# Plain fp32 for the small products of a hybrid block (scores, values, gates), a mask added in PSUM, and other banks and steps for statistics

## The chip, the cores and the metric

The kernel runs on one core of a Trainium2 chip. The metric is the time of one execution on the device, in microseconds. Engines: TensorE (PE, matrix products; "PEld" are its weight loads), VectorE (DVE), ScalarE (ACT), GpSimd (POOL) and SyncE (SP, which issues the transfers). Each engine executes its own instructions in order; semaphores order the engines among each other.

## The reference

One layer of a hybrid block over 512 tokens (S) of width 2048 (D), in fp32. Its core, cut:

```python
mod = c_act @ w_ada + b_ada                       # six vectors: shift, scale, gate, twice
h = rms_norm(x, g_mix) * (1 + sc1) + sh1
xr, yr, q, k, v, f_logit = split(h @ w_in)        # 1024, 1024, 1024, 1024, 1024, 8
# recurrent group: 8 blocks of 128 channels
u = causal_depthwise_conv(xr)                     # 4 taps
r, i = sigmoid(block_diag(u, w_a) + b_a), sigmoid(block_diag(u, w_x) + b_x)
a = exp(-8 * r * softplus(-lam)); y_rec = scan(a, sqrt(1 - a * a) * (i * u)) * gelu(yr)
# attention group: 8 heads of 128, query blocks of 128
s = rms_norm(q) @ rms_norm(k).T / sqrt(128) + cum_q - cum_k     # cum: cumulative log of the forget gate
p = softmax(where(causal, s, -inf)); y_att = p @ v
x = x + gt1 * (concat(rms_norm(y_rec), rms_norm(y_att)) @ w_out)
h2 = rms_norm(x, g_ffn) * (1 + sc2) + sh2
gate, up = split(h2 @ w_up); x = x + gt2 * ((silu(gate) * up) @ w_down)
```

## The kernel before

**Split products.** Nearly every product is made from fp32 values that are split in two: a high part, which ACT copies in the rounded type fp32r (`R(...)` reinterprets an access as fp32r), and a low part, which DVE or POOL makes by subtraction. `mm` (L187) issues one fp32r product; a full product is three of them: high by high, high by low, low by high. Weights stream in through `raw` (two buffers), and are split into `whi`/`wlo` (three buffers each) on ACT (L182) and DVE (L183). A few small products are plain fp32: the sums and spreads of the statistics (L247, L256), the transposes (L470, L508), the bias sums.

**Stages.** In order: `w1` (the projection to `xr`, with the product for the modulation vectors `ada`/`adf` as long DVE steps L134/L144 beside it); the statistics of x (`rstd_x`: sums by products with ones, four columns copied, a power on POOL, a spread by products with the identity); `yr0` (a feature-major group, four PSUM banks); heads `h0` to `h7` (`tm_group`: 16 k-tiles x four token tiles x three products into 384 columns, 392 for head 0); `yr1`; `wo0` to `wo3` (output projection); `up0`, `up1` (two standard groups of the up projection) and then the rest of it in "fast chunks" `uf4` to `uf43`, whose weights and moving operands are sums of pieces made on DVE; `dn` (down projection).

**Attention inside projections.** Attention of head h runs beside the projection of head h+1 (of head 7 beside `yr1`): its steps are hooked after given k-tiles by `ATT_STEPS` (statistics of q and k, transposes of q and k, the four score blocks two by two, the transposes of the probabilities, the value products). A score block b is the product of 128 queries with (b+1) x 128 keys. Its bias is made ahead on ACT from the cumulative forget logits (L484), POOL adds the causal mask `dmask` to the last 128 columns (L485), and DVE's L498 adds the score from PSUM and takes the row's maximum (`nm`). The recurrent group works in pairs of blocks (`rec_pair`) hooked the same way in the stages of heads 3 to 6: `conv` loads a block of `xr` back, scales and filters it to `u`, splits u, loads the gates' weights `gw` and splits them to `gpg`; the gates and what follows (`carry`) run in the next head's stage.

**PSUM.** Eight banks of 128 x 512: four `acc` (projections), three `misc` and one `rg`. yr0 takes the four acc banks, as head 0 after it. Before a bank is taken again, its contents must have been copied out (L382 for yr0, L445 to L449 for a head, L498 for scores).

**Order.** A scheduler in the build orders each engine's instructions from priorities, from the program's order and from its own estimate of when operands are there; on the chip an engine then runs its list in order. `ahead` raises the priority of weight loads and splits, `EVAC` that of the copies out of a head's banks. In wo0, the statistics of the attention output are summed and spread at step 2, those of the recurrent output at step 5 (`MIXREC`), and `mix_rec` then scales the recurrent blocks. At the end of each standard up group `up_fin` takes the bias's sums and writes the activations (`up_out`).

## Time and profile before

| | us |
|---|---|
| Median of three runs | 2206.79 (2200.26 to 2207.86) |
| Profiled execution | 2206.86 |
| Its span | 2205.1 |
| TensorE busy | 2108.9 (96%) |
| VectorE busy | 1590.6 (72%) |
| ScalarE busy | 879.4 (40%) |
| GpSimd busy | 222.6 (10%) |

The profile is one execution recorded by the hardware. Its page lists busy time by engine, the span in 40 slices, the chain of work that ended last, and groups of instructions; the trace behind it answers for single stretches: windows (busy time of each engine in a stretch), waits (what an engine stood still for, by the event that ended the wait), lines (groups of equal instructions) and a timeline. [...] Ends of pipelined products are modelled, so the price of a product is read from start to start. A plain fp32 product leaves two records in the trace for one instruction.

### The profile page before, as it was taken

Reading aid. Unit: us, or ns where it says so; the run is one execution under the profiler, and the core shown is the slowest. Engines: PE = TensorE matmul, PEld = TensorE weight load, DVE = VectorE, ACT = ScalarE, POOL = GpSimd, SP = SyncE. Lnnn points to the kernel's source line nnn. Section 1 sums busy time; section 2 is a strip of 40 time slices with the busy share of each in tenths; the row PEclk is TensorE's granted clock in tenths of the full one; section 3 lists DMA queues with packets and bytes.
Section 4 is the critical chain, followed back from the end, with each engine's and each line's share of the span. In section 5 each row is a group of like instructions: output and inputs, shape, how many; then the busy total and the mean of one; then the engine's idle time right before and its main releaser. Section 6 shows DMA issues by size and latency. Waiting matters only on the chain.

```text
span 2205.1 us, 32703 instructions
## 1 busy us (share of the span) xinstructions
PE 2108.9 (96%) x12785; PEld 1915.9 (87%) x12785; DVE 1590.6 (72%) x2407; ACT 879.4 (40%) x1238; POOL 222.6 (10%) x169
## 2 busy tenths in 40 slices
PE   8987988888989999899999999999999999999999
PEld 6767887887878888799999999999999888888887
DVE  8997679887877779988888888888888443322332
ACT  5522336656543335544444444444444222221111
POOL 2260113333212310000000000000000000000000
PEclk9998999999999999999999999999999999999999
DMA  9968666665667862343444344443434985554443
GB/s 322 319 209 286 198 225 202 197 218 172 224 211 253 278 218 103 112 144 117 134 134 135 124 129 139 131 128 125 144 126 136 335 310 195 177 198 138 154 158 109
DMA packets 133021, 406.05 MB, mean 184 GB/s; under 512 B 14561, under 2 KB 19841, under 8 KB 123138
## 3 DMA queue, kind: packets, MB, share of 16 engines
q1 hardware_dynamic: 132866, 403.96, 54.6%
q8 instruction: 100, 1.64, 0.3%
q14 instruction: 55, 0.45, 0.1%
HBM read 361.15 MB, written 42.75 MB: 183 GB/s over the span
## 4 chain that ended last, share of the span: by engine, by line
PE 73%; DVE 12%; DMA 8%; ACT 3%; issue 2%; POOL 1%; SPq 0%; DVEq 0%; POOLq 0%; ACTq 0%
PE dn_0p L187 5%; PE dn_3p L187 5%; PE dn_2p L187 5%; PE dn_1p L187 5%; DMA ada<-in_adaT 2%; PE up0p L187 2%; PE wo2p L187 2%; PE wo3p L187 2%; PE wo1p L187 2%; DMA bw<-in_w 2%; DVE adf L144 2%; DVE ada L144 1%; PE uf5p L962 1%; PE uf42p L962 1%; PE uf35p L962 1%
## 5 line engine op out<-in xcount | busy, mean ns | idle before, releaser
L134 DVE SCALAR_TENSOR_TENSOR ada<-ada,c_b 128x1024 f32<-128x1024 f32 x128 | 165.9, 1307 | 46.3 <-DMA ada<-in_adaT 45.9
L183 DVE TENSOR_TENSOR uq_0tl<-uq_0r,uq_0th 128x1024 fp32r<-128x1024 f32 x40 | 49.0, 1225 | 63.9 <-ACT uq_0th L182 63.9
L182 ACT ACTIVATE uq_0sh<-uq_0r 128x1024 fp32r<-128x1024 f32 x40 | 42.5, 1061 | 89.5 <-PE uf23p L962 2.3
L183 DVE TENSOR_TENSOR uq_0al<-uq_0r,uq_0ah 128x1024 fp32r<-128x1024 f32 x40 | 49.0, 1225 | 40.1 <-ACT uq_0ah L182 40.1
L182 ACT ACTIVATE uq_1th<-uq_1ra 128x1024 fp32r<-128x1024 f32 x40 | 42.5, 1061 | 72.7 <-DVE uq_1ra L942 2.7
L182 ACT ACTIVATE uq_0th<-uq_0r 128x1024 fp32r<-128x1024 f32 x40 | 42.4, 1061 | 72.4 <-DVE uq_0r L942 1.9
L182 ACT ACTIVATE uq_1sh<-uq_1rb 128x1024 fp32r<-128x1024 f32 x40 | 42.5, 1062 | 70.5 <-PE uf43p L962 2.4
L182 ACT ACTIVATE uq_1ah<-uq_1ra 128x1024 fp32r<-128x1024 f32 x40 | 42.5, 1061 | 60.7 <-issue 59.2
L182 ACT ACTIVATE uq_0ah<-uq_0r 128x1024 fp32r<-128x1024 f32 x40 | 42.4, 1060 | 50.4 <-issue 46.8
L144 DVE SCALAR_TENSOR_TENSOR adf<-adf,c_b 128x1024 f32<-128x1024 f32 x32 | 56.4, 1763 | 2.3 <-DMA adf<-in_adaT 2.3
L183 DVE TENSOR_TENSOR uq_1tl<-uq_1ra,uq_1th 128x1024 fp32r<-128x1024 f32 x40 | 49.0, 1225 | 10.4 <-ACT uq_1th L182 10.4
L187 PE MATMUL w1p<-hph,w1h 128*128 128x512 f32 x128 | 48.7, 408 | 6.2 <-ACT hph L327 6.1
L187 PE MATMUL w1p<-hpl,w1h 128*128 128x512 f32 x128 | 52.1, 407 | 1.9 <-DVE hpl L328 1.6
L183 DVE TENSOR_TENSOR uq_0sl<-uq_0r,uq_0sh 128x1024 fp32r<-128x1024 f32 x40 | 49.0, 1226 | 4.0 <-ACT uq_0sh L182 0.4
L183 DVE TENSOR_TENSOR uq_1sl<-uq_1rb,uq_1sh 128x1024 fp32r<-128x1024 f32 x40 | 49.0, 1225 | 2.8 <-ACT uq_1sh L182 0.6
L187 PE MATMUL w1p<-hph,w1l 128*128 128x512 f32 x128 | 50.9, 398 | 0.0
L183 DVE TENSOR_TENSOR uq_1al<-uq_1ra,uq_1ah 128x1024 fp32r<-128x1024 f32 x40 | 48.6, 1216 | 0.1
L574 DVE SCALAR_TENSOR_TENSOR ba<-bw,sh,ba 128x512 f32<-128x512 f32 x45 | 33.2, 751 | 20.4 <-DMA bw<-in_w 17.0
L144 DVE SCALAR_TENSOR_TENSOR ada<-ada,c_b 128x1024 f32<-128x1024 f32 x32 | 41.2, 1287 | 3.7 <-DMA ada<-in_adaT 3.7
L183 DVE TENSOR_TENSOR dn_1l<-dn_2r,dn_1h 128x1024 fp32r<-128x1024 f32 x11 | 13.5, 1226 | 38.0 <-ACT dn_1h L182 38.0
L183 DVE TENSOR_TENSOR dn_1l<-dn_0r,dn_1h 128x1024 fp32r<-128x1024 f32 x11 | 13.5, 1226 | 37.6 <-ACT dn_1h L182 37.6
L183 DVE TENSOR_TENSOR dn_0l<-dn_2r,dn_0h 128x1024 fp32r<-128x1024 f32 x11 | 13.5, 1225 | 37.6 <-ACT dn_0h L182 37.6
(13854 smaller groups left out, 8430.9 us busy)
## 6 DMA issues: line engine op xcount, KB each, us to landing
ada<-in_adaT SPq DMA_DIRECT2D x160, 512.0 KB, 5.2
uq_0r<-in_wups SPq DMA_DIRECT2D x80, 512.0 KB, 4.1
uq_1ra<-in_wups SPq DMA_DIRECT2D x40, 512.0 KB, 4.0
uq_1rb<-in_wups SPq DMA_DIRECT2D x40, 512.0 KB, 3.2
adf<-in_adaT SPq DMA_DIRECT2D x32, 512.0 KB, 5.6
actd<-ach SPq DMA_DIRECT2D x44, 256.0 KB, 2.0
actd<-acl SPq DMA_DIRECT2D x44, 256.0 KB, 4.0
dn_0r<-in_wdown SPq DMA_DIRECT2D x11, 1024.0 KB, 4.9
```

The source lines that it names most:

```text
L134: nc.vector.scalar_tensor_tensor(out=t, in0=t, scalar=1.0, in1=cs, op0=ALU.mult, op1=ALU.mult, accum_out=ac)
L144: nc.vector.scalar_tensor_tensor(out=t, in0=t, scalar=1.0, in1=c_b[:, cs], op0=ALU.mult, op1=ALU.mult, accum_out=ada_acc[j][:, hf, i:i + 1])
L182: nc.scalar.activation(R(hi[:, :n]), raw_ap, AF.Copy)
L183: tail_lo.append(nc.vector.tensor_sub(R(lo[:, :n]), raw_ap, hi[:, :n]).ins)
L187: nc.tensor.matmul(ps, lhsT=R(l), rhs=R(r), start=start, stop=stop)
L574: nc.vector.scalar_tensor_tensor(out=ba[j], in0=src, scalar=s1, in1=ba[j], op0=ALU.mult, op1=ALU.add)
L962: nc.tensor.matmul(m[p], lhsT=R(w[:, ks]), rhs=R(x), start=first and p in opens, stop=last, skip_group_check=True)
```

## The change

- Scores: the transposed q and k are copied once, by ACT, and each score block is one plain fp32 product; the causal mask is added in PSUM by a second product, identity by mask, both rounded to fp32r once at the kernel's start. The DVE subtraction (L473) and the POOL mask addition (L485) go.
- Value products: v and the transposed probabilities are copied once and multiplied as plain fp32; the DVE subtractions L449 and L512 go.
- Gates: plain fp32 products of the loaded weights and u; the splits of both go.
- Steps: attention's steps come one to two k-tiles later (`ATT_STEPS`), with the score blocks in two pairs at steps 8 and 9; the forget logits' sums of head 0 at step 4, not 2.
- Banks: the w1 banks are copied out in another order, the statistics of x use acc banks, and yr0 uses the three misc banks and the rg bank.
- wo0: both sums at step 1, both spreads at step 4.
- The epilogue of the second standard up group (`up_out`) is issued after the first fast chunk's first half.

```diff
 YR0_AHEAD = 80
-MIXREC = 5
+FORGET_STEP = 4
+MIXREC_STEPS = (1, 4)
...
+    nc.scalar.activation(R(ident_r), ident, AF.Copy)
+    nc.scalar.activation(R(dmask_r), dmask, AF.Copy)
...
-    for f in range(8):
+    for f in (4, 5, 6, 7, 0, 1, 2, 3):
...
-    rstd_x = rstd_bcast(ssq_x, D, "rstd_x")
+    rstd_x = rstd_bcast(ssq_x, D, "rstd_x", bank=acc)
...
-    yr0 = fm_group(wyr[0], list(range(KT)), hp, "yr0", hooks=hk0, ahead=YR0_AHEAD)
+    yr0 = fm_group(wyr[0], list(range(KT)), hp, "yr0", hooks=hk0, ahead=YR0_AHEAD,
+                   ps=[misc(f"yr0p{f}") for f in range(3)] + [rgp("yr0p3")])
...
-            nc.scalar.activation(R(vh[:, t, :]), ps[t][:, 256:384], AF.Copy)
-            nc.vector.tensor_sub(R(vl[:, t, :]), ps[t][:, 256:384], vh[:, t, :])
+            nc.scalar.activation(v[:, t, :], ps[t][:, 256:384], AF.Copy)
...
-                nc.scalar.activation(R(hi), pt, AF.Copy, scale=g)
-                nc.vector.scalar_tensor_tensor(out=R(lo), in0=pt, scalar=g, in1=hi, op0=ALU.mult, op1=ALU.subtract)
+                nc.scalar.activation(zt, pt, AF.Copy, scale=g)
...
-                nc.gpsimd.tensor_add(bt[:, bs], bt[:, bs], dmask)
...
-            mm(ps[:, :n], qh[:, bs], kh[:, :n], True, False)
-            mm(ps[:, :n], qh[:, bs], kl[:, :n], False, False)
-            mm(ps[:, :n], ql[:, bs], kh[:, :n], False, True)
+            nc.tensor.matmul(ps[:, :n], lhsT=qT[:, bs], rhs=kT[:, :n], start=True, stop=False)
+            mm(ps[:, bs], ident_r, dmask_r, False, True)
...
-            nc.scalar.activation(R(hi[:, qs]), pt[:, qs], AF.Copy)
-            nc.vector.tensor_sub(R(lo[:, qs]), pt[:, qs], hi[:, qs])
+            nc.scalar.activation(pT[:, qs], pt[:, qs], AF.Copy)
...
-            mm(po[:, qs], vh[:, kb, :], hi[:, qs], kb == 0, False)
-            mm(po[:, qs], vh[:, kb, :], lo[:, qs], False, False)
-            mm(po[:, qs], vl[:, kb, :], hi[:, qs], False, kb == NT - 1)
+            nc.tensor.matmul(po[:, qs], lhsT=v[:, kb, :], rhs=st[kb][:, qs], start=kb == 0, stop=kb == NT - 1)
...
-            UH[n], UL[n] = split_to(u, f"u{n}", "c")
...
-            nc.scalar.activation(R(gh), gw, AF.Copy)
-            nc.gpsimd.tensor_sub(R(gl), gw, gh)
-            GP[n] = (gh, gl)
+            GP[n] = gw
...
-            mm(ps, gh[:, cs], UH[n], True, False)
-            mm(ps, gh[:, cs], UL[n], False, False)
-            mm(ps, gl[:, cs], UH[n], False, True)
+            nc.tensor.matmul(ps, lhsT=GP[n][:, cs], rhs=U[n], start=True, stop=True)
...
-    ATT_STEPS = (None, 5, 7, 7, 7, 7, 10, 11, 12, 12, 13, 13, 14, 14)
+    ATT_STEPS = (None, 6, 8, 8, 9, 9, 12, 12, 13, 13, 14, 14, 15, 15)
...
-            add(hk, 2, frest)
+            add(hk, FORGET_STEP, frest)
...
+    def mix_sums():
+        att_sums()
+        rec_sums()
 
     def mix_rec():
-        ratio = rstd_bcast(ssq_rec, D_REC, "ratio", times=att_rms)
+        st_att.append(att_spread())
+        ratio = rec_spread()
...
-            add(hk, 2, rstd_a)
-            add(hk, MIXREC, mix_rec)
+            add(hk, MIXREC_STEPS[0], mix_sums)
+            add(hk, MIXREC_STEPS[1], mix_rec)
...
-        up_out(gi, ps, bup, range(2))
+        return lambda: up_out(gi, ps, bup, range(2))
...
-        up_fin(gi, ps, bu_acc)
+        up_last = up_fin(gi, ps, bu_acc)
+        if gi < STD - 1:
+            up_last()
...
+            if f == 2 * STD and c == 0:
+                up_last()
```

What the scheduler makes of it, at three places. A row names line, operation, output <- inputs (with buffer numbers) and shape; line numbers are those of the respective kernel.

TensorE in head 1's attention, which runs beside head 2's projection (`s_0` to `s_3` are the four score blocks, `h2p` the banks of head 2). Before:

```order
L187 MATMUL s_0_2474<-qkh_1_2419,qkh_0_2410 128x128
L187 MATMUL s_0_2474<-qkl_1_2420,qkh_0_2410 128x128
L187 MATMUL s_0_2474<-qkh_1_2419,qkl_0_2411 128x128
L187 MATMUL s_1_2484<-qkh_1_2419,qkh_0_2410 128x256
L187 MATMUL s_1_2484<-qkl_1_2420,qkh_0_2410 128x256
L187 MATMUL s_1_2484<-qkh_1_2419,qkl_0_2411 128x256
L187 MATMUL s_2_2494<-qkh_1_2419,qkh_0_2410 128x384
L187 MATMUL s_2_2494<-qkl_1_2420,qkh_0_2410 128x384
L187 MATMUL s_2_2494<-qkh_1_2419,qkl_0_2411 128x384
L187 MATMUL s_3_2504<-qkh_1_2419,qkh_0_2410 128x512
L187 MATMUL s_3_2504<-qkl_1_2420,qkh_0_2410 128x512
L187 MATMUL s_3_2504<-qkh_1_2419,qkl_0_2411 128x512
```

and of the changed kernel the same place:

```order
L495 MATMUL s_0_2450<-qkT_1_2399,qkT_0_2392 128x128
L192 MATMUL s_0_2450<-dmask_r,ident_r 128x128
L495 MATMUL s_1_2459<-qkT_1_2399,qkT_0_2392 128x256
L192 MATMUL s_1_2459<-dmask_r,ident_r 128x128
...
L192 MATMUL h2p_2255<-h_0h,hl_1375 128x384
L495 MATMUL s_2_2489<-qkT_1_2399,qkT_0_2392 128x384
L192 MATMUL s_2_2489<-dmask_r,ident_r 128x128
L495 MATMUL s_3_2498<-qkT_1_2399,qkT_0_2392 128x512
L192 MATMUL s_3_2498<-dmask_r,ident_r 128x128
```

Each block's three products became two, with the mask as the second one, and twelve head products now stand between the second and the third block.

TensorE at the gates of block 5 (of blocks 0 to 7), in head 6's stage (`gp` the banks of the two gates, `h6p` those of head 6). Before, after 135 products of the stage:

```order
L187 MATMUL h6p_4240<-h_1h,hl_1487 128x384
L187 MATMUL gp_0_4282<-u5h,gpg_4051 128x512
L187 MATMUL gp_0_4282<-u5l,gpg_4051 128x512
L187 MATMUL gp_0_4282<-u5h,gpg_4051 128x512
L187 MATMUL gp_1_4286<-u5h,gpg_4051 128x512
L187 MATMUL gp_1_4286<-u5l,gpg_4051 128x512
L187 MATMUL gp_1_4286<-u5h,gpg_4051 128x512
L187 MATMUL h6p_4241<-h_1h,hh_1486 128x384
```

and of the changed kernel, after 12 and after 24 products of head 6:

```order
L192 MATMUL h6p_4019<-h_0h,hl_1047 128x384
L603 MATMUL gp_0_4038<-u_3675,gw_3680 128x512
L603 MATMUL gp_1_4040<-u_3675,gw_3680 128x512
L192 MATMUL h6p_4016<-h_0h,hh_1072 128x384
...
L192 MATMUL h6p_4019<-h_0h,hl_1073 128x384
L603 MATMUL gp_0_4054<-u_3826,gw_3831 128x512
L603 MATMUL gp_1_4056<-u_3826,gw_3831 128x512
L192 MATMUL h6p_4016<-h_1h,hh_1114 128x384
```

The six products of the second block became two and stand 111 products nearer to the stage's begin.

DVE at the seam between the second standard group (`up1p`) and the first fast chunk (`uq_`; `te7l` is the last piece of its moving operand, `sg`, `su`, `acl` belong to the epilogue of the group before). Before:

```order
L845 TENSOR_TENSOR td7l<-ta_7824,td7h 128x512
L891 TENSOR_TENSOR sg_0_7851<-up1p_7468,rstd_7218 128x512
L845 TENSOR_TENSOR te7l<-tb_7825,te7h 128x512
L893 TENSOR_TENSOR su_0_7852<-up1p_7470,rstd_7218 128x512
L891 TENSOR_TENSOR sg_1_7864<-up1p_7469,rstd_7218 128x512
L894 SCALAR_TENSOR_TENSOR sg_0_7851<-su_0_7852,bup_7844,sg_0_7851 128x512
L893 TENSOR_TENSOR su_1_7865<-up1p_7471,rstd_7218 128x512
L894 SCALAR_TENSOR_TENSOR sg_1_7864<-su_1_7865,bup_7844,sg_1_7864 128x512
L882 TENSOR_TENSOR acl_7858<-sg_0_7851,ach_7857 128x512
L937 TENSOR_TENSOR uq_0cl<-uq_0r,uq_0ch 128x512
L882 TENSOR_TENSOR acl_7871<-sg_1_7864,ach_7870 128x512
```

and of the changed kernel:

```order
L838 TENSOR_TENSOR tc7l<-h2x_7471,tc7h 128x512
L932 TENSOR_TENSOR uq_0cl<-uq_0r,uq_0ch 128x512
L847 TENSOR_TENSOR tb_7477<-ta_7476,h2x_7471 128x256
L934 TENSOR_TENSOR uq_0r<-uq_0r 128x512
L838 TENSOR_TENSOR td7l<-ta_7476,td7h 128x512
L935 TENSOR_TENSOR uq_0r<-uq_0r 128x512
L838 TENSOR_TENSOR te7l<-tb_7477,te7h 128x512
L936 TENSOR_TENSOR uq_0r<-uq_0r 128x512
L188 TENSOR_TENSOR uq_0sl<-uq_0r,uq_0sh 128x1024
L937 TENSOR_TENSOR uq_0r<-uq_0r 128x512
L884 TENSOR_TENSOR sg_0_7614<-up1p_7120,rstd_6870 128x512
L886 TENSOR_TENSOR su_0_7615<-up1p_7122,rstd_6870 128x512
```

The epilogue's steps stood ahead of `uq_0cl`; now `uq_0cl` and the further splits of the chunk's weights stand ahead of them.


## Rows read from the trace of the kernel before

**Rows 1.** The page's first line (span and instructions), and of its first part the line of TensorE's matmuls and the engines beside them: busy time, share of the span, number of instructions.
```profile
span 2205.1 us, 32703 instructions
...
PE 2108.9 (96%) x12785; PEld 1915.9 (87%) x12785; DVE 1590.6 (72%) x2407; ACT 879.4 (40%) x1238; POOL 222.6 (10%) x169
```

**Rows 2.** Windows of core 0 (from:to and length in us; then busy us and number of records of PE, PE's weight loads, DVE, ACT and POOL; the mean granted clock of TensorE as a share of full speed; the DMA engines' busy share; GB/s). In time these are the pause between yr0 and head 0, head 0, heads 1 to 7 but for the last's end, and everything from within wo0 to the end.
```profile
163.40:173.40 10.00, 0.09 (x1) 0.02 (x1) 6.79 (x12) 2.94 (x4) 0.00 (x0) 0.69 0.76 258
173.40:213.00 39.60, 36.26 (x192) 35.96 (x193) 30.27 (x54) 11.12 (x18) 0.00 (x0) 0.93 0.86 289
213.00:560.00 347.00, 303.61 (x1662) 287.13 (x1663) 275.21 (x495) 181.52 (x332) 99.81 (x82) 0.94 0.62 205
...
664.00:2205.00 1541.00, 1528.18 (x9902) 1403.83 (x9900) 1045.80 (x1465) 566.18 (x693) 44.42 (x25) 1.00 0.49 164
```

**Rows 3.** Waits of TensorE over the whole span (waiting tile and line <- engine, tile and line that ended the wait: us in total, number of times, longest one).
```profile
PE s L187 <- DVE qkl L473: 16.6, 5, 4.5
PE h0p L187 <- DVE yr L382: 9.9, 1, 9.9
PE s L187 <- ACT qkh L472: 6.5, 2, 3.7
PE uf4p L962 <- ACT uq_0ch L936: 4.8, 1, 4.8
PE gp L187 <- ACT gpg L604: 4.4, 1, 4.4
PE rstd_attb L256 <- POOL rstd_attt L236: 4.2, 1, 4.2
PE s L187 <- DVE nm L498: 3.5, 3, 2.9
PE h1p L187 <- DVE z L409: 3.3, 1, 3.3
PE qkt L470 <- DVE qk L463: 3.3, 3, 1.2
PE po L187 <- ACT pth L511: 2.9, 2, 2.1
...
PE h5p L187 <- DVE vl L449: 1.7, 1, 1.7
...
PE po L187 <- DVE ptl L512: 1.5, 1, 1.5
PE gp L187 <- POOL gpg L605: 1.5, 1, 1.5
...
PE uf4p L962 <- DVE uq_0cl L937: 1.2, 1, 1.2
```

**Rows 4.** Timeline of TensorE at head 0's score blocks (start, duration, engine, line, operation, out<-in, weights and moving shape; in brackets the idle time ahead and what ended it): the first product of a block into 128, 256 and 384 columns, the head product that follows the third block, then the three products into 512 columns.
```profile
235.41 0.22 PE L187 MATMUL s<-qkh,qkh 128*128 128x128 f32 x1
...
235.69 0.33 PE L187 MATMUL s<-qkh,qkh 128*128 128x256 f32 x1
...
236.09 0.34 PE L187 MATMUL s<-qkh,qkh 128*128 128x384 f32 x1
...
236.62 0.33 PE L187 MATMUL h1p<-h_0h,hh 128*128 128x384 f32 x1
...
244.00 0.50 PE L187 MATMUL s<-qkh,qkh 128*128 128x512 f32 x1 [2.88 <-DVE nm L498]
244.34 0.39 PE L187 MATMUL s<-qkl,qkh 128*128 128x512 f32 x1
244.57 0.40 PE L187 MATMUL s<-qkh,qkl 128*128 128x512 f32 x1
```

**Rows 5.** The same view where the statistics of x are spread (plain fp32, four products written in eight records), with the product that follows, and below it the group of the kernel's first products (number of records: shortest, median and longest duration in ns, first and last start; shapes).
```profile
115.23 1.16 PE L256 MATMUL rstd_xb<-ident,rstd_xt 128*128 128x128 f32 x8 [1.69 <-POOL rstd_xt L236]
116.14 0.48 PE L187 MATMUL yr0p<-hph,yr_0h 128*128 128x512 f32 x1
...
L103 PE MATMUL cps<-cr,ones x4: 1055/1056/1188, 2.4 to 5.1; 1*128 1x512 f32 x4
```

**Rows 6.** Groups of weight loads on TensorE: of the plain spread of the statistics of x, and of a split head product of head 1.
```profile
L256 PEld LDWEIGHTS rstd_xb<-ident,rstd_xt x8: 186/190/191, 115.2 to 116.0; 128*128 128x128 f32 x8
...
L187 PEld LDWEIGHTS h1p<-h_0h,hh x32: 187/188/331, 213.0 to 254.1; 128*128 128x128 f32 x32
```

**Rows 7.** A group of DVE's instructions in 210 to 640 us (durations as in rows 5) and one of POOL's (number of instructions, busy us and mean ns of one, idle time before them and what ended it): the low part of the transposed q, and the addition of the causal mask.
```profile
L473 DVE SCALAR_TENSOR_TENSOR qkl<-qkt,gqs,qkh x8: 736/742/748, 232.7 to 590.2; 128x512 fp32r<-128x512 f32 x8
...
L485 POOL TENSOR_TENSOR bt<-bt,dmask 128x128 f32<-128x128 f32 x32 | 28.0, 895 | 55.5 <-ACT bt L484 55.4
```

**Rows 8.** Timeline of DVE between yr0 and head 1: the copies out of the four yr0 banks, and a later step of the modulation's product that waits for its transfer.
```profile
172.57 2.48 DVE L382 TENSOR_TENSOR yr<-yr0p,rstd_x 128x512 f32<-128x512 f32 x4
...
190.25 1.23 DVE L144 SCALAR_TENSOR_TENSOR ada<-ada,c_b 128x1024 f32<-128x1024 f32 x1 [1.90 <-DMA ada<-in_adaT]
```

**Rows 9.** Timeline at the first fast chunk: DVE's split of `uq_1s`, and the first of TensorE's products that takes up `uq_1s`.
```profile
926.16 1.22 DVE L183 TENSOR_TENSOR uq_1sl<-uq_1rb,uq_1sh 128x1024 fp32r<-128x1024 f32 x1
...
929.95 0.28 PE L962 MATMUL uf4p<-td4h,uq_1sh 128*128 128x256 f32 x1
```

**Rows 10.** Timeline of TensorE at the gates of the last pair but one, and of the waits of ACT in 210 to 640 us the line of the reloaded conv input.
```profile
492.02 0.80 PE L187 MATMUL gp<-u5h,gpg 128*128 128x512 f32 x1 [4.40 <-ACT gpg L604]
...
ACT xrl L592 <- POOL xrl L591: 21.0, 5, 7.2
```

41 lines of the change are left out of this document (19 added, 22 removed).

## The prediction

> **What bounds the kernel now.** I read the page's first part first: TensorE (PE) is busy 2108.9 of 2205.1 us, 96% [rows 1]. So only two things can move the time: the length of PE's own products, and the few stretches in which PE stands still. The windows say where those lie [rows 2]: from 664 us to the end PE works 1528 of 1541 us; in 213 to 560 us (head projections with attention between them) only 304 of 347, at a mean granted clock of 0.94; from 163 to 173 us next to nothing. VectorE (DVE) works 275 of those 347 us, 79%. The table of waits names what PE stood still for [rows 3]: score products for the split copies of q and k (16.6 + 6.5 us) and for the softmax's first DVE step `nm` (3.5), head 0 for `yr` (9.9), the fast chunk for `uq_0c` (4.8 + 1.2), gates for `gpg` (4.4 + 1.5), a spread of statistics for `rstd_attt` (4.2), and smaller ones. The change touches nearly every one, so the sum goes wait by wait. Durations come from the profiled execution: 2206.86 us, its span plus 1.76, practically the median of the runs.
>
> **What plain products cost.** No product of these shapes stands in the trace as plain fp32, so the price comes from others. Split: the three products into 128, 256 and 384 columns take 0.28, 0.40 and 0.53 us from start to start, one into 512 about 0.23 [rows 4]; the four score blocks of a head so take 0.28 + 0.40 + 0.53 + 3 x 0.23 = 1.90 us. Plain: the spread of `rstd_xb` is four plain products into 128 columns and leaves eight records; from its start to the next product's is 0.91 us, 0.114 a record [rows 5]. Two records into 128 columns are 0.23 us, 1.78 ns a column: the 1280 columns of a head's scores take 2.28 us, a gate of 512 columns 0.91 against 0.69 split. The other end of the range is `cps` at the kernel's start: two plain products into 512 columns in four records of 1.056 us [rows 5], before the clock had risen. If that were their price later too, a plain product into 512 columns would cost 2.11 us, 1.42 more than split. I take the first, as its records lie among products at the full clock.
> Scores: +0.38 us a head, and four mask products into 128 columns at 0.11: +0.44. Value products, with the same columns: +0.38. Eight heads: 8 x 1.20 = 9.6. Gates: 16 x 0.22 = 3.5. Together **+13** us on PE. At the dear end it is scores and values 5 x 512 columns a head, 40, and 16 gates: 56 x 1.42 = 80, with the masks 83.
>
> A plain product also loads its weights twice. The loads of `rstd_xb` take 186 to 191 ns, those of a split head product 188 in the median [rows 6], beside the products before them. For the 160 plain records (64 of scores, 64 of values, 32 of gates) I take nothing; laid bare, they would be 160 x 0.188 = 30 us. [...]
>
> **What it takes away: scores.** A score now waits for one ACT copy of each transposed operand, and no more for a DVE subtraction of 0.74 us behind it [rows 7] that queues in a busy DVE. In PE's order 24 head products still stand between transposes and first score; 12 new ones stand between the second and third block, so that DVE can free a bank for it. The POOL addition of the mask, 0.9 us each [rows 7], leaves the front of the softmax. The waits on `qkl`, `qkh` and `nm` are 26.6 us [rows 3]; ACT's queue stays, so I leave 5: **-21.5** (-10 to -26).
> Transposes behind `qk` (3.3): one k-tile later, **-2.5**. Value products behind `pth` and `ptl` (2.9 + 1.5): the copy stays, the subtraction goes, **-3**. Behind `vl` (1.7) and, after head 0, `z` (3.3): the copies that free the four banks stay, the `vl` subtraction goes, **-3.5** [rows 3].
>
> **Gates.** 5.9 us behind `gpg` [rows 3], which an ACT copy and a POOL subtraction make; both go, and the weights come straight from a transfer: **-4** (the gates move too; see the fourth rival).
>
> **yr0 and head 0.** Head 0 waits 9.9 us [rows 3] because it takes the banks of yr0, which DVE drains in 2.48 us, late in its queue [rows 8]. In after yr0 has other banks, and head 0 can begin some 10 us earlier. But DVE's queue (the `ada` steps and the splits of head 0's weights) does not get shorter by that, and waits for transfers itself, 1.9 us before the step at 190 us [rows 8]; the DMA share there is 0.86 [rows 2]. Head 0 will catch up with its splits: **-4** (-0.5 to -8).
>
> **wo0.** The attention's sums now have 78 head products, not 59, before the next statistics' step, and both spreads come together: of 4.2 us, **-3.5** (-4.2 to +2, if the second spread now waits).
>
> **Fast chunk.** 6.0 us behind `uq_0c` [rows 3]. DVE now makes `uq_0cl` ahead of the epilogue of the group before. But PE next wants `uq_1s`: its DVE split ended at 927.4, and PE took it up at 929.95 [rows 9], so a PE that is 6 us early stands there 3.5 us before that split's end: by an unmoved queue 2.5 us are left. The epilogue's steps move behind, but other splits that PE needs stand ahead of `uq_1sl` too: **-1.5** (0 to -6).
>
> **The clock.** A mean of 0.94 over 347 us [rows 2] is 347 x 0.06 = 21 us less than the full level would give; the score behind the wait for `nm` took 0.50 us, the next 0.40 [rows 4], so the low level follows the pauses. Some of it falls in the pauses, where it costs nothing. If 12 us of it cost work and two thirds of the pauses go, **-8** (0 to -14).
>
> **The sum.** -21.5 - 2.5 - 3 - 3.5 - 4 - 4 - 3.5 - 1.5 - 8 = -51.5; +13; net -38.5: 2206.9 - 38.5 = 2168 us. The waits that I left out (each below 2.5 us) will rather shrink than grow, which I take as one more: **2167**. With scores, clock, head 0 and the fast chunk each at their small ends, the other terms (16.5) as they are: 2206.9 + 13 - 10 - 0.5 - 16.5 = 2193; at their great ends: 2206.9 + 13 - 26 - 14 - 8 - 6 - 16.5 = 2149.
>
> **The rivals.**
> First, waits come back in about half (chance 0.21). DVE still has three quarters of these stages, and `qkT` and `pT` wait in ACT's queue behind the copies of the weights. Against it, the DVE steps by which PE waited for most of its 16.6 us are gone altogether. Gains of 30, price 13: 2190 (2181 to 2196).
>
> Second, weight loads of plain records come onto the path (0.05): 30 us on the forecast, 2197. Against it: rows 6. [...]
>
> Third, little moves (0.07): PE, released, meets the next late operand everywhere, because transfers and DVE beneath are the true bound. For it: DVE at 79%. Against it: a DMA share of 0.62 in the same window [rows 2]; neither is full. 2196 to 2211.
>
> Fourth, slower, by gates (0.05). PE runs in order, and the gates of a second block now stand after product 24 of a stage; for head 6 before had them after 135, so 111 products of about 0.17 us, 19 us, later. The wait at 492.02 [rows 10] was there. If conv's `u` is not there so early, all that is queued on PE behind stands: head products, transposes, scores, and with them the engines that wait for these. The conv's input `xrl` kept ACT waiting up to 7.2 us [rows 10]; one such wait in each of four stages, 29 us, and the scores' 21.5 back, as the same DVE is late for both: -39.5 + 29 + 21.5 = +11, 2218. It decides from 40 us of such stalls on. Against it: the splits of `u` and of the gates' weights, an ACT, a DVE and a POOL step, no longer stand before a gate.
>
> Fifth, the dear price of plain products (0.02): 70 us on the forecast, 2237.
>
> **How the numbers follow.** The forecast has 0.60, its own range 2149 to 2181; the rivals 0.21, 0.05, 0.07, 0.07. In perhaps a tenth of the first case's chance all gains and more come together, below 2146. I give 2146 to 2197: that leaves out about 0.05 below and 0.13 above. Half a per cent, 11 us, is about what a measurement of this kernel tells from no change. Faster by more: 0.60 + 0.21, and 0.05 for loads that are bare in part only and for the best of the third case: 0.86. Within: 0.08, the rest of these two and the mildest of the fourth. Slower: 0.06.
>
> **What would show it.** In the table of waits no `qkl`, `ptl`, `vl`, `gpg`, and below 6 us in all at the scores; head 0 below 6 us at its begin or in its splits; nothing above 1 us at the spreads of wo0; the stretch from head 1's first product to yr1 shorter by 25 to 30 us at a clock of 0.97 or more; plain records starting 0.1 us apart at 128 columns, 0.45 at 512. Wrong would be a wait of gates on `u` or `gw` above 5 us a stage, `qkT` or `pT` in the place of `qkl` and `ptl` at more than 10 us, or plain products well above 1.78 ns a column.

## The result and the profile after

The changed kernel takes 2190.43 us in the median of five runs (2185.2 to 2194.53), the kernel before 2205.32 in five runs (2200.26 to 2207.86): the ratio is 0.9934, with an interval of 0.9913 to 0.9956. A second measurement, beside 29 runs of before, gave 0.9951 (0.9930 to 0.9971). I take the mean of both, 0.9943, where a version is compared with the changed kernel below. The gain is 11 to 15 us where 39.5 were forecast; the time lies within the range given, and at the place of the first rival, 2190.

The two profiles that are compared first are 21.7 us apart (2206.86 and 2185.2), since one lies near the slow end of its runs and the other at the fast end. A control pair of profiles, taken on one chip, is 11.6 us apart (spans 2200.7 and 2189.1). Where it matters, both pairs are given.

The page's first lines for the changed kernel, answering to [rows 1]:

```profile
span 2183.5 us, 32375 instructions
...
PE 2114.4 (97%) x12737; PEld 1911.2 (88%) x12737; DVE 1560.4 (71%) x2319; ACT 873.1 (40%) x1224; POOL 187.3 (9%) x129
```

PE itself works 5.5 us longer than before and the span is 21.6 us shorter, so 27 us of standing still are gone. Next its windows, answering to [rows 2], columns as there: head 0, heads 1 to 7, yr1, wo0, the rest.

```profile
164.40:209.10 44.70, 35.43 (x194) 33.80 (x192) 36.35 (x63) 12.84 (x19) 0.00 (x0) 0.98 0.87 301
209.10:554.50 345.40, 318.52 (x1671) 293.09 (x1672) 258.83 (x450) 184.95 (x339) 73.55 (x50) 0.94 0.65 216
554.50:606.10 51.60, 50.99 (x233) 40.83 (x231) 36.96 (x65) 22.86 (x40) 5.63 (x4) 1.00 0.70 243
606.10:663.70 57.60, 51.80 (x225) 41.81 (x226) 46.30 (x69) 23.08 (x36) 9.00 (x8) 0.94 0.63 210
663.70:2183.00 1519.30, 1511.16 (x9825) 1389.77 (x9823) 1032.39 (x1439) 557.78 (x682) 40.55 (x25) 1.00 0.48 163
```

Head 0 begins at 164.4 us, 9.0 us earlier than in [rows 2], and ends only 3.9 us earlier. In heads 1 to 7 PE still stands still for 27 of 345 us, at the clock of 0.94 that it had before. The table of waits, answering to [rows 3], says for what:

```profile
PE s L495 <- DVE nm L499: 10.3, 4, 3.1
PE pt L509 <- DVE bt L503: 8.2, 5, 2.4
PE w1p L192 <- ACT hph L333: 6.1, 6, 4.9
PE h1p L192 <- DVE z L416: 5.9, 1, 5.9
PE h3p L192 <- ACT v L454: 3.1, 1, 3.1
PE h0p L192 <- DVE h_1l L188: 2.9, 3, 1.2
...
PE wo0p L192 <- ACT mx0h L180: 2.1, 1, 2.1
...
PE wo0p L192 <- DVE mx2l L181: 1.9, 1, 1.9
...
PE s L495 <- ACT qkT L477: 1.8, 1, 1.8
```

The names of the splits are gone, as they must be. The new names are `nm`, the softmax's first DVE step, which frees the bank that the fourth score block needs, and `bt`, the softmax's last DVE step, without which the transposes `pt` can't begin. What the first wait looks like in DVE's timeline, while PE has its third block at 375.50 and gets to the fourth at 379.42:

```profile
374.65 1.21 DVE L139 SCALAR_TENSOR_TENSOR ada<-ada,c_b 128x1024 f32<-128x1024 f32 x1
...
375.80 0.74 DVE L593 SCALAR_TENSOR_TENSOR u<-xrl,vec,u 128x509 f32<-128x509 f32 x1
376.46 0.68 DVE L544 SCALAR_TENSOR_TENSOR ge<-ge,yrl 128x512 f32<-128x512 f32 x1
377.06 1.21 DVE L139 SCALAR_TENSOR_TENSOR ada<-ada,c_b 128x1024 f32<-128x1024 f32 x1
...
378.20 0.95 DVE L188 TENSOR_TENSOR h_0l<-h4r,h_0h 128x768 fp32r<-128x768 f32 x1
```

DVE does not rest: modulation steps (`ada`), the conv (`u`), the output gate (`ge`) and a weight split stand ahead of the softmax's first step (L499, 0.28 us from 379.08), for which PE waits 3.04 us. That is the first theory: DVE is late with its whole list, and a split that no longer has to be waited for only lets PE meet the next step of that list. Its rivals: the new steps are badly placed; plain products are dear; a bank is missing.

### The profile page after: what moved, and what is told of

Read it like the earlier page. It is cut to its first block, busy times and chain, and to the rows that moved or that the text cites. A ratio compares the mean times of both kernels' runs of the same rounds, so it can differ in the third digit from the quotient of the medians.

```text
span 2183.5 us, 32375 instructions
## 1 busy us (share of the span) xinstructions
PE 2114.4 (97%) x12737; PEld 1911.2 (88%) x12737; DVE 1560.4 (71%) x2319; ACT 873.1 (40%) x1224; POOL 187.3 (9%) x129
## 4 chain that ended last, share of the span: by engine, by line
PE 77%; DVE 12%; DMA 6%; issue 3%; ACT 2%; POOL 1%; SPq 0%; DVEq 0%; POOLq 0%; ACTq 0%
PE dn_0p L192 5%; PE dn_3p L192 5%; PE dn_2p L192 5%; PE dn_1p L192 5%; PE up0p L192 2%; PE wo3p L192 2%; PE wo2p L192 2%; PE wo1p L192 2%; DVE adf L149 2%; PE wo0p L192 2%; DMA ada<-in_adaT 2%; PE yr1p L192 1%; PE h3p L192 1%; DMA bw<-in_wyr 1%; DVE ada L149 1%
## 5 line engine op out<-in xcount | busy, mean ns | idle before, releaser
L188 DVE TENSOR_TENSOR uq_1tl<-uq_1ra,uq_1th 128x1024 fp32r<-128x1024 f32 x40 | 49.0, 1226 | 10.3 <-ACT uq_1th L187 10.2
L571 DVE SCALAR_TENSOR_TENSOR ba<-bw,sh,ba 128x512 f32<-128x512 f32 x45 | 34.2, 769 | 23.8 <-DMA bw<-in_w 12.5
L192 PE MATMUL w1p<-hph,w1l 128*128 128x512 f32 x128 | 50.7, 396 | 0.0
L188 DVE TENSOR_TENSOR dn_1l<-dn_2r,dn_1h 128x1024 fp32r<-128x1024 f32 x11 | 13.5, 1226 | 38.0 <-ACT dn_1h L187 38.0
L188 DVE TENSOR_TENSOR dn_0l<-dn_2r,dn_0h 128x1024 fp32r<-128x1024 f32 x11 | 13.5, 1225 | 37.6 <-ACT dn_0h L187 37.6
L188 DVE TENSOR_TENSOR dn_1l<-dn_0r,dn_1h 128x1024 fp32r<-128x1024 f32 x11 | 13.5, 1225 | 37.4 <-ACT dn_1h L187 37.4
```

The lines of the kernel that those rows point to most:

```text
L188: tail_lo.append(nc.vector.tensor_sub(R(lo[:, :n]), raw_ap, hi[:, :n]).ins)
L192: nc.tensor.matmul(ps, lhsT=R(l), rhs=R(r), start=start, stop=stop)
L571: nc.vector.scalar_tensor_tensor(out=ba[j], in0=src, scalar=s1, in1=ba[j], op0=ALU.mult, op1=ALU.add)
```

## The experiments

### Which part of the change does it

Two runs undo or isolate the products, one undoes the steps:

```diff
# old steps (from the changed kernel)
-ATT_STEPS = (None, 6, 8, 8, 9, 9, 12, 12, 13, 13, 14, 14, 15, 15)
+ATT_STEPS = (None, 5, 7, 7, 7, 7, 10, 11, 12, 12, 13, 13, 14, 14)
-FORGET_STEP = 4
+FORGET_STEP = 2
# plain products only: the kernel before, with head_evac, attention, conv and gate of the changed kernel
# steps and banks only: the changed kernel, with those functions of the kernel before
```

> The changed kernel with the attention's steps of before (and the forget logits' sums at step 2 again). Theory 'softmax': the split's waits were replaced by waits on the softmax's DVE steps (nm 10.3, bt 8.2 us), which come wherever the steps stand, because DVE is late: then the sum of the waits of scores and probability transposes stays between 12 and 24 us, and the time within 5 us of the changed kernel (2185 to 2195). Rival 'steps': the later and tighter steps themselves make the waits; then nm and bt fall below 8 us together and the time to 2182 or less.

> The kernel before with plain scores, value products and gates and the mask in PSUM, and nothing else of the change (old steps, old banks, old places of statistics and epilogue). Theory 'softmax': the split waits (qkl, qkh, gpg, ptl, vl: some 31 us) go, about half returns at nm and bt, the products cost about 8 us: 6 to 12 us below before, head 0's wait on yr at 9 to 10 us as before. Rival 'price': plain products cost as much as they free, the time is within 3 us of before or above it. Rival 'steps': 15 us or more below before, since the old steps were the better ones.

> The changed kernel with split products again (scores, values, gates, the mask on POOL), but its steps, banks, statistics and epilogue. Theory 'softmax': only what lies outside the attention remains, 4 us at head 0 and 4 at the fast chunk; the waits on qkl and qkh stay above 12 us; 4 to 9 us below before. Rival 'steps': the later steps cost; same as before or slower. If e2 and e5 add to the 15 us of the whole change, the parts are independent; if they add to more than 20, they compete for the same waits.

Measured: old steps 0.9979 (0.9965 to 0.9993), plain products alone 1.0022 (1.0009 to 1.0036), steps and banks alone 1.0010 (0.9997 to 1.0023). Neither half of the change gains; both together do. With the old steps the waits of scores and probability transposes come to 25.8 us, a little above the 12 to 24 expected, so the later steps don't make these waits. Then two more and two controls, to fill the table:

> The kernel before, once more, as a control beside the next three on one chip: same as before within 0.2%, and a profile of its own, whose stretch from head 1 to wo0 (412.5 us in the first one) says how far two profiles of one kernel differ. All theories: 408 to 416.

> The changed kernel, once more, as a control: 12 to 18 us below before (0.9913 to 0.9956 in the first measurement), head 1 to wo0 397 us within 5.

> The kernel before with the other banks of yr0, the new places of wo0's statistics and the deferred epilogue, but split products and old attention steps. Theory 'sum of places': these three are worth 4 us at head 0, 0 at wo0 and 4 at the fast chunk whatever the attention does: 6 to 10 us below before. Rival 'interaction': what they free is lost again in the attention of the next heads, as in the run with old steps: within 3 us of before.

> The kernel before with plain products and the new attention steps (and the forget sums at step 4), but its old banks, statistics and epilogue. Theory 'pair': plain products and the later, paired steps help only together (plain with old steps was 3 us slower than before, split with new steps 1 us slower): together 8 to 14 us below before in the heads, so 2186 to 2193 where before is 2200. Rival 'places': the gain of the whole change comes from banks, statistics and epilogue; then this one is within 4 us of before.

"Stretch" is from the first product of head 1 to the first of wo0, in one profile; "idle" is its length less PE's busy time there; "places" are yr0's banks, wo0's statistics and the deferred epilogue.

| products | steps | places | ratio to before | stretch, us | idle, us |
|---|---|---|---|---|---|
| split | old | old | 1 (control 0.9996) | 412.5, 410.4 | 47.9, 49.5 |
| plain | old | old | 1.0022 | 406.4 | 35.9 |
| plain | new | old | 0.9985 (0.9973 to 0.9998) | 402.0 | 35.1 |
| split | old | new | 0.9980 (0.9968 to 0.9992) | 406.1 | 43.5 |
| split | new | new | 1.0010 | 412.0 | 50.1 |
| plain | old | new | 0.9979 | 405.8 | 34.2 |
| plain | new | new | 0.9934, 0.9951 | 397.1, 401.8 | 27.5, 32.8 |

Plain products cost 0.2% with the old steps and old places and gain 0.67% with new steps and new places (1.0010 to 0.9943). The new steps cost 0.3% with split products (0.9980 to 1.0010) and gain 0.36 to 0.37% with plain ones. So the steps are not badly placed: they are right for plain products alone. The places are worth 0.2% with split products (4.4 us, where 6 to 10 or at most 3 were expected) and 0.4% with plain ones. Plain products and new steps without the places gain 0.15%, some 3 us, where theory 'pair' had 8 to 14: by the bounds set for that run its rival 'places' holds, and most of the whole change's 0.57% comes only when the places are added. As each ratio has an interval of 0.12 to 0.22% to either side, a single difference of 0.2% in this table is at the edge of what can be told.

Why plain products at the old steps give nothing, the waits of that run say:

```profile
PE s L492 <- DVE nm L496: 16.6, 6, 5.7
...
PE s L492 <- ACT qkT L474: 7.8, 3, 4.0
```

24.4 us at the scores, against 26.6 in [rows 3]: with four blocks hooked to one k-tile, the fourth one's wait for a bank had been hidden behind the wait for the split. Head 3's attention, beside head 4, shows it, first in the kernel before, then in that run (a score product and the wait ahead of it):

```profile
383.51 0.58 PE L187 MATMUL s<-qkh,qkh 128*128 128x256 f32 x1 [4.09 <-DVE qkl L473]
```

```profile
383.20 2.07 PE L492 MATMUL s<-qkT,qkT 128*128 128x512 f32 x2 [5.70 <-DVE nm L496]
```

Before, PE waits 4.09 us for the split and then has no wait at the fourth block; with plain products it reaches the fourth block without that and waits 5.70 us there. With the waits for ACT's copies ahead of these it is 7.8 us before and 7.1 in that run. For the control pair of before and changed kernel the same can be added up, first before, then changed:

```profile
PE s L187 <- DVE qkl L473: 13.9, 5, 4.3
...
PE s L187 <- DVE nm L498: 5.6, 3, 4.7
PE s L187 <- ACT qkh L472: 3.9, 1, 3.9
```

```profile
PE s L495 <- DVE nm L499: 11.1, 5, 4.3
PE pt L509 <- DVE bt L503: 9.9, 5, 3.8
...
PE s L495 <- ACT qkT L477: 3.5, 1, 3.5
```

23.4 us became 24.5; with the 1.5 us of `bt` that before had too, 24.9 became 24.5. The scores gave nothing net here; what the stretch gained (8.6 us in this pair) came from gates, value products and transposes of q and k.

### A bank, or DVE

```diff
# fourth block in the rg bank
-            ps = misc(f"s{h}_{b}")
+            ps = rgp(f"s{h}_{b}") if b == NT - 1 else misc(f"s{h}_{b}")
# other k-tiles for the modulation steps
-H_ADA = (3, 4, 7, 10, 14)
+H_ADA = (1, 3, 4, 5, 14)
# 24 of 30 modulation blocks into the output projection
-H_ADA = (3, 4, 7, 10, 14)
-WO_ADA = 5
+H_ADA = (14,)
+WO_ADA = 10
```

> The changed kernel with the fourth score block in the rg bank in place of the third misc bank, so that it need not wait for the first block's DVE step to free one. Theory 'bank': the waits on nm (10 to 11 us) fall below 4, nothing takes their place, the stretch from head 1 to wo0 (397 to 402 us) shrinks by 6 to 10. Theory 'DVE late': the softmax as a whole is late, so what nm loses comes back at pt behind bt (8.2 to 9.9 now): the sum of both stays above 14 us, the stretch within 4 us.

> The changed kernel with the modulation steps of heads 3 to 8 hooked at other k-tiles (1, 3, 4, 5, 14 in place of 3, 4, 7, 10, 14): the same work, fewer of it among the softmax's steps in DVE's order. Theory 'DVE late by position': nm and bt together lose 4 to 10 us of 18.5 to 21. Theory 'DVE late by amount' and theory 'bank': within 4 us of the changed kernel.

> The changed kernel with 24 of the 30 modulation blocks (two DVE steps of 1.2 us and two transfers each) moved out of the head stages into the output projection. Theory 'DVE late': nm and bt fall below 10 us together, the waits of head products and gates too, the stretch from head 1 to wo0 falls from 397 to 402 us to 380 to 390; the time of the whole falls by 5 to 15 us unless the output projection, whose DVE gets 12 us more in each of four stages of 43.5, becomes longer. Theory 'bank': nm and bt stay within 4 us; only the product stretch is unchanged.

With the further bank no wait on `nm` is left, and this stands in its place:

```profile
PE pt L509 <- DVE bt L503: 24.8, 13, 5.9
```

The stretch is 401.9 us, the ratio 0.9953 (0.9938 to 0.9968): the bank only moved the wait. Other k-tiles for the modulation moved it too (nm 4.7, bt 9.2, but `v` and `qkT` more; 402.0 us, 0.9946). With most of the modulation taken away, most of it goes; the stretch of that run, and its waits:

```profile
211.10:589.20 378.10, 364.38 (x1901) 330.45 (x1901) 232.58 (x413) 208.11 (x378) 65.12 (x54) 0.96 0.49 164
```

```profile
PE up0p L192 <- ACT up_0h L187: 59.2, 1, 59.2
...
PE pt L509 <- DVE bt L503: 6.8, 4, 3.1
```

378.1 us, some 21 less than the changed kernel, idle 13.7, and of the waits on `nm` one of 1.8 us is left. The price came due elsewhere: the output projection's DVE fell behind, and up0 waited 59.2 us for it, so that the whole took 2254.6 us (1.0248). A bank is not the cause; that DVE is late fits, but with the blocks their transfers were moved too.

Is it DVE's own work, or its waits for the modulation's transfers? Two runs keep one and drop the other, and a third takes a smaller dose:

```diff
# transfers without steps
-nc.vector.scalar_tensor_tensor(out=t, in0=t, scalar=1.0, in1=cs, ...)
+nc.vector.scalar_tensor_tensor(out=t[:, :16], in0=t[:, :16], scalar=1.0, in1=cs[:, :16], ...)
# steps without transfers
-nc.sync.dma_start(out=t, in_=adaT[...])
-nc.vector.scalar_tensor_tensor(out=t, in0=t, ...)
+nc.vector.scalar_tensor_tensor(out=t, in0=cs, ...)
# smaller dose: H_ADA = (3, 10, 14), WO_ADA = 7
```

> The changed kernel with every transfer of the later modulation blocks in place, but each of their DVE steps made on 16 of 1024 columns (the product of the modulation vectors for the gates and for the second norm is thereby left out for the other columns). Theory 'amount of DVE work': head 1 to wo0 falls to 375 to 388 us, as without the blocks. Theory 'transfers': DVE still waits 15 us for these transfers in its queue, and the stretch stays at 393 or more.

> The opposite: the DVE steps of these blocks at full length, but on a vector that is already on the chip, without their transfers (which leaves the product with the modulation weights out). Theory 'amount of DVE work': the stretch loses only the waits for these transfers, 393 to 400 us. Theory 'transfers': it falls to 388 or less. If both this run and the one before fall by more than 10 us, DVE's length and its waits for transfers add up.

> The changed kernel with 12 of the 30 modulation blocks of the head stages moved to the output projection (two more in each of its four stages, 4.9 us of DVE where some 11 are free), a smaller dose than the 24 that made the output projection late. Theory 'DVE late': head 1 to wo0 falls from 397 to 402 us to 386 to 394, wo1 to wo3 stay at 43.5, the whole time to 2178 to 2186 where before is 2201. Rival: the output projection is late again, or the heads do not gain: 2188 to 2195.

The stretch with transfers but without steps, and with steps but without transfers:

```profile
210.70:587.30 376.60, 361.61 (x1902) 327.19 (x1903) 230.93 (x514) 206.25 (x378) 66.66 (x54) 0.97 0.68 231
```

```profile
210.50:599.20 388.70, 363.72 (x1901) 328.98 (x1901) 295.18 (x514) 207.56 (x378) 79.54 (x54) 0.97 0.40 135
```

Without the steps 376.6 us (ratio of the whole 0.9823), without the transfers 388.7 (0.9889), where the changed kernel has 397.1 and 401.8. (Two executions each.) The steps weigh 20 to 25 us, the transfers 8 to 13, and as the run without both in most of the heads (378.1) is not shorter than the first, they don't add up. The waits say the same: first without the steps, then without the transfers.

```profile
PE pt L509 <- DVE bt L503: 6.2, 7, 3.0
...
PE s L495 <- DVE nm L499: 1.8, 1, 1.8
```

```profile
PE s L494 <- DVE nm L498: 12.1, 5, 3.2
PE pt L508 <- DVE bt L502: 7.2, 5, 2.4
```

Without the steps 8.0 us are left of these two waits, without the transfers 19.3, about as many as in the changed kernel (18.5 and 21.0). So these waits are made by DVE's own work. Of what the run without transfers gains, 5 to 6 us are PE's own time (363.7 us where the changed kernel has 369.6 and 369.0), at a mean granted clock of 0.97 for 0.95 and 0.96. The smaller dose brought the heads the gain (381.3 us) but cost the output projection more (wo2 54.2, wo3 50.4 us in place of 43.5, up0 57.9 for 46.2): 1.0023. My expectation there was wrong: wo2 and wo3 have no 5 us to spare, though DVE is busy for only 30 to 34 of 43.5 us there.

### The seams, and wo0

```diff
# all copies of q, k, v on ACT
-            if t % 2:
-                nc.vector.tensor_copy(out=qk[:, t, :], in_=ps[t][:, 0:256])
-            else:
-                nc.scalar.activation(qk[:, t, :], ps[t][:, 0:256], AF.Copy)
+            nc.scalar.activation(qk[:, t, :], ps[t][:, 0:256], AF.Copy)
# wo0's statistics at the old steps 2 and 5, each with its sum and spread
```

> The changed kernel with all copies of q, k and v out of a head's banks on ACT (before: those of tiles 1 and 3 of q and k on DVE). Theory 'queue': PE's waits at the head seams (z 5.9, v 4.0 us) and the slow clock behind the one of head 3 come from DVE's copies standing behind modulation and bias steps in DVE's queue, not from the amount of copying: then the waits on v fall below 1.5 us, head 3's stage loses 6 to 9 us (53.6 now), and the time falls by 6 to 12 us. Rival 'amount': ACT, with 16 copies more, is late instead (h_0h, qkT, pT); time the same or longer by up to 5 us.

> The changed kernel with wo0's statistics where they were (attention's sums and spread at step 2, the recurrent ones at step 5). Theory 'mix pieces': the wait on rstd_attt (3 to 4 us) only moved to the mix pieces mx0h and mx2l (4.0 us in the changed kernel), and wo0 got 1 to 3.6 us longer: with the old places wo0 takes 54 to 57 us instead of 57.5 to 58, the whole time is 0 to 3 us shorter than the changed kernel's. Rival 'spread': the new places save the 4 us as forecast and wo0's length comes from elsewhere: then 60 us or more.

With the copies on ACT the waits on `v` are gone, the one on `z` after head 0 is not (5.4 us), and others took their place (`qkT` 5.2): the time is the changed kernel's, 0.9936 (0.9913 to 0.9960). Head 3's stage took 50.6 us, 3 less and not the 6 to 9 expected. That `v`, a copy of ACT, waits for DVE shows in the changed kernel's timeline of ACT:

```profile
299.87 0.28 ACT L454 ACTIVATE v<-h2p 128x128 f32<-128x128 f32 x1 [4.41 <-DVE qk L451]
```

What `z` waits for stands in the changed kernel's DVE timeline; PE had finished head 0's products at 203:

```profile
203.73 0.75 DVE L571 SCALAR_TENSOR_TENSOR ba<-bw,sh,ba 128x512 f32<-128x512 f32 x1 [2.29 <-DMA bw<-in_w]
...
208.17 0.75 DVE L571 SCALAR_TENSOR_TENSOR ba<-bw,sh,ba 128x512 f32<-128x512 f32 x1 [1.54 <-DMA bw<-in_w]
208.84 0.16 DVE L416 TENSOR_TENSOR z<-h0p,bfb 128x8 f32<-128x8 f32 x1
```

The bias steps `ba`, each waiting for its transfer, stand ahead of the copies. Head 0 arrives early and finds DVE where it was. The runs with the other banks but split products show how much of the 9 us is given back; with old steps its waits are

```profile
PE h1p L188 <- DVE z L412: 5.7, 1, 5.7
...
PE h0p L188 <- DVE h_1l L184: 4.7, 2, 2.8
```

and from yr0's first product to head 1's it takes 102.7 us, with new steps 101.7, where the kernel before has 103.8 and 102.1. With plain products the runs in the new banks take 98.7 to 103.1 us and the two in the old ones 100.8 and 99.0. So practically all of the 9 us is given back.

With the old places wo0 takes 61.6 us (61.6 also in the run of plain products and new steps with old places), with the new ones 57.5 and 58.0; before, with split products, it took 56.6 and 54.4. So my theory here, that the new places only moved the wait, falls: they save 4 us, as the prediction had it. They do so only with plain products and new steps: with split products and old steps wo0 takes 54.5 us in the new places and 56.6 and 54.4 in the old, with plain products and old steps 57.3 and 58.5. And with plain products and new steps wo0 had become 5 to 7 us longer. I put that down to PE, which now comes to wo0 ahead of the other engines; no run shows it by itself, but in the run without the modulation's DVE steps wo0 takes 50.7 us, so DVE's work sets its length too. The whole time with the old places was 0.9962 (0.9949 to 0.9975).

### Relief for DVE at a smaller price

```diff
# norms of q and k on ACT
-                nc.vector.tensor_tensor(z, z, ss[...].broadcast_to([P, NT, P]), ALU.mult)
+                for t in range(NT):
+                    nc.scalar.activation(z[:, t, :], z[:, t, :], AF.Copy, scale=ss[:, 4 * a + t:4 * a + t + 1])
# and the softmax's last scaling on ACT
-            nc.vector.tensor_scalar_mul(p[:, :n], p[:, :n], sm)
+            nc.scalar.activation(p[:, :n], p[:, :n], AF.Copy, scale=sm)
# and the fourth score block in the rg bank, as above
```

> The changed kernel with the scaling of q and k by their norms on ACT (8 copies of 128 columns a head) in place of two DVE steps of 0.69 us a head, behind which DVE's queue also stood still for POOL's statistics (13.5 us in all). DVE is relieved of about 11 us of steps and 13 of waits in head 1 to wo0. Theory 'DVE's time': that stretch falls by 8 to 15 us (from 397 to 402), by the measure of 24 modulation blocks (58 us of steps) for 20 to 24, the whole to 2178 to 2185 where before is 2201. Rival 'ACT': the scaling is late on ACT, with 64 more steps there; qkt waits for it and the time is that of the changed kernel or longer.

> The same with the softmax's last scaling (32 DVE steps of 0.38 us) on ACT too, 12 us less on DVE. Theory 'DVE's time': pt no longer waits for DVE's bt but the whole chain is shorter by what DVE's queue held: another 3 to 8 us off. Rival 'ACT': ACT's queue (copies of weights, exponentials) holds the scaling up; the waits on bt move to ACT with the same 7 to 10 us, nothing gained over the run before.

> The last version (both scalings on ACT) with the fourth score block in the rg bank as well. There PE waits 18.0 us at nm and 5.3 at pt. Theory 'DVE's time': the bank moves the wait again, the sum of nm and pt stays above 16 us and head 1 to wo0 at 392 to 400 (396.4 now). Theory 'bank': with a relieved DVE the bank is what is left, nm falls without a rise at pt, the sum below 12 us, the stretch to 385 to 391, the ratio to before 0.987 to 0.990.

Measured: 0.9958 (0.9946 to 0.9970) with a stretch of 405.0 us; 0.9919 (0.9905 to 0.9932) with 396.4; 0.9931 (0.9911 to 0.9950) with 396.6. The first gained nothing: PE's wait on `nm` rose to 16.8 us, although DVE was busy 13 us less there than in the control. So DVE's busy time alone doesn't tell PE's wait. DVE's own waits in the stretch, first of the control of the changed kernel, then of this run, show where the relief went:

```profile
DVE h_1l L188 <- ACT h_1h L187: 17.9, 8, 4.5
DVE qk L468 <- POOL ss L241: 13.5, 8, 2.0
```

```profile
DVE h_1l L188 <- ACT h_1h L187: 29.4, 12, 4.0
```

The 13.5 us behind POOL's statistics are gone, and the waits of the weight splits for ACT, which now has the scaling, rose by 13.1 (with `h_0l`, 25.7 to 38.8). That is the rival 'ACT', in another place than I had expected it. It doesn't settle the matter alone: with both scalings on ACT these waits are 42.2 us, and the stretch is 8.6 us shorter than in the first run. Of that 6.8 are PE's own time (369.9 to 363.1), at a mean granted clock of 0.97 for 0.95. With both scalings on ACT the waits read

```profile
PE s L496 <- DVE nm L500: 18.0, 6, 5.7
...
PE pt L510 <- ACT bt L504: 5.3, 4, 3.1
```

and with the bank, once more, `nm` is gone and `bt` has all of it:

```profile
PE pt L510 <- ACT bt L504: 21.6, 13, 3.1
```

The version with both scalings on ACT has the lowest ratio of the complete kernels, with 2186.68 us beside 2205.67 for before, and is faster than before by 0.7 to 0.95%; against the changed kernel (0.9934 and 0.9951, measured beside other runs of before) its advantage of 0.2% is within the intervals and not shown.

## Why the prediction was right or wrong

**Plain products: right, the sum with the clock by luck.** Four records of two gates in the changed kernel, and the next product:

```profile
351.58 1.88 PE L603 MATMUL gp<-u,gw 128*128 128x512 f32 x4
352.89 0.74 PE L192 MATMUL h4p<-h_0h,hh 128*128 128x384 f32 x1
```

From start to start it is 1.31 us; the records themselves begin 0.43 apart, and the last one's time falls into the 0.74 of the next product. That makes 0.86 us a gate where the prediction had 0.91. PE's own time in the stretch rose by 5.0 us (364.5 to 369.6) and in the control pair by 8.1 (360.9 to 369.0); forecast were 13 of price less 8 of clock, 5. That this agrees is luck: the mean granted clock of the stretch is the same in both kernels (0.95 and 0.95, in the control pair 0.96 and 0.96), so the 5 to 8 us are nearly all price, smaller than forecast, and the clock gave next to nothing. The dear price and bare weight loads, the fifth and second rivals, are excluded by that: they would have added 70 and 30. The dear price, that of `cps`, belongs to the kernel's begin: there the split products of `w1` into 512 columns start 0.43 us apart too (12.84 to 17.11 us in the trace of before), as score products do at 386.67 to 387.95 us, where the granted clock is 0.50, and from 17.11 us on 0.23; the granted clock itself reads 1.00 from 2.3 to 20 us. The weight loads of the plain scores, values and gates, two to a product, take 189, 189 and 190 ns in the median in the changed kernel.

**Clock: too hopeful.** Forecast -8. The stretch's mean granted clock stayed at 0.95 to 0.96, since waits stayed. In before it reads 0.50 from 168 to 173 us, in the pause that begins at 163.4, and from 379 to 388, with waits of 3.7 and 4.1 us that end at 378.95 and 383.51, but 1.00 from 244 to 246, behind the 2.88 us wait for `nm`: so the 0.50 us of that score [rows 4] is not the low clock for which the prediction took it. Where the waits went, in the run without the modulation's steps, it is 0.97 and PE's own time is 361.6 us, 7 to 8 below the changed kernel's. How dear a wait is shows head 3 of the changed kernel, where the 3.1 us behind `v` end at 300.2; windows as above:

```profile
295.80:300.00 4.20, 1.30 (x9) 0.98 (x7) 3.99 (x8) 0.13 (x1) 0.00 (x0) 0.90 0.82 268
300.00:303.00 3.00, 2.80 (x9) 2.72 (x10) 1.55 (x3) 2.97 (x7) 0.72 (x1) 0.50 0.96 266
303.00:306.00 3.00, 3.00 (x11) 3.00 (x10) 3.00 (x4) 0.24 (x1) 1.39 (x1) 0.50 0.80 316
306.00:309.00 3.00, 3.00 (x22) 3.00 (x21) 1.26 (x3) 0.85 (x1) 2.71 (x2) 1.00 0.73 212
```

After it six us pass at a granted clock of 0.50, in which 20 records are worked off instead of some 40 (22 in the next three us): the wait costs its 3.1 us and, by this estimate, about 3 more. Head 3's stage took 53.6 us against 45.4 before (control 53.3 against 47.6).

**Scores: the step that failed.** "The waits on `qkl`, `qkh` and `nm` are 26.6 us; ACT's queue stays, so I leave 5: -21.5." Left were 12.1 us of these and 8.2 of `bt`, 20.3 in all where before had 27.6 with its `bt`; in the control pair 24.5 against 24.9: a gain of 7 or none. The prediction's own sign fell with it: from head 1's first product to yr1 the time is 10.9 us shorter (control 2.7), not 25 to 30. The step took the named releaser for the cause. `qkl` was the last of several things that DVE had to do; the softmax behind it stood in the same queue, and the wait for a bank, hidden until then, came out. The second half of the step, that twelve products between the second and third block "let DVE free a bank", came true for `nm` alone: at the old steps it takes 16.1 to 16.6 us, at the new ones, with all places new, 10.3 to 11.1. But `bt` rises from 1.8 us to 8.2 and 9.9, so that both together stay the same (17.9 and 18.4 against 18.5 and 21.0). What the new steps gain at the scores is at `qkT`, 7.8 and 7.9 us at the old steps and 1.8 and 3.5 at the new ones.

**Value products, transposes, gates: right.** 4.4, 3.3 and 5.9 us of waits on `pth`/`ptl`, `qk` and `gpg` went altogether; 3, 2.5 and 4 were forecast. No gate waited for `u` or `gw`, though the second pair stood up to 111 products earlier: the fourth rival is excluded.

**Stage ends: wrong in sign.** Forecast -3.5; `z` went from 3.3 to 5.9 us (control 1.5 to 5.8) and `v` stands at 4.0 (3.1 and 0.9) where `vl` had 3.2 (control 2.1 and 3.3). The subtraction went, but the copies' place behind bias and modulation steps in DVE's list remained, and PE came earlier.

**yr0 and head 0: right by luck, -4.0** (103.8 to 99.8 us for both; control 102.1 to 99.6). The mechanism was that the banks give 10 us and the splits take some 6 back. The begin came 9 us earlier, but what the splits and `z` take back is about as much: with the other banks and split products both stages take 102.7 and 101.7 us, with plain products the old banks do as well as the new ones (100.8 and 99.0). What shortened these stages in the two pairs is open; the two profiles of before differ by 1.7 us there.

**wo0: right by its place, given back by the stage.** -3.5 forecast; the new places save 4 beside plain products and new steps, the stage as a whole is 0.9 us longer (control 3.6).

**Fast chunk: too small.** -1.5 forecast, -4.0 measured from its begin to the down projection (815.8 to 811.8 us; control 815.3 to 811.8), inside the bounds; the standard group ahead of it became 0.8 and 0.6 us longer, so about 3 are left. PE's waits for the splits there fell from 6.0 to 1.7 us: the ones that stand ahead of `uq_1sl` came nearly in time.

**The rivals.** The first, waits that come back in about half, is what happened, with its 2190; it was given 0.21 against 0.60. Of the two reasons given for it, ACT's queue counts little (`qkT` 1.8 us, 3.5 in the control, `pT` none); DVE's load is nearly all. The third, that transfers and DVE beneath are the bound, was half true: without the modulation's DVE steps the stretch falls by 20 to 25 us.

**What stays open:** how far 11 us of DVE's norm steps (and 13 of its waits) went without any gain because DVE then waited 13 us more for ACT, and how far because its list was ordered anew. The order of DVE's list, which the scheduler makes anew each time, differs between these runs, and no run held it fixed.

## What to carry to other kernels

A wait names the last thing that was missing, not the only one. Before a wait on a busy engine's step is booked as gain, take the step out of that engine's queue in thought and see what PE meets next in the same queue; here, with the engine busy for three quarters of the stage, 7 us or none came of 26.6. Work that is off the bound, such as a matrix-vector product hooked into the projections, can set the time through its engine's order: here its steps weigh 20 to 25 us in that stretch, and all that the change removed 9 to 15. And a term whose number comes true isn't shown by that: runs with and without its step decide, as they did for yr0's banks.

## What was not expected of the hardware

Plain fp32 products into 512 columns cost 0.86 us (from start to start, above) against 0.69 for three rounded ones [rows 4], and their double weight loads show no price of their own: PE's time in the stretch rose by 5 to 8 us, where the loads laid bare would have added 30 by the prediction's estimate. And executions of one and the same kernel on one chip differ by up to 0.8% (2192.7 to 2209.4 us in 28 runs of before), more than the whole change is worth, so two single profiles can say up to twice what the medians say.
